# HGRN projections as seven block products for eight over half the rows, and the residual stream kept in DRAM

## The chip, the cores and the metric

One core of one Trainium2 chip runs the whole kernel. The metric is the device time of one execution in microseconds; the kernel before takes 2060.48 us (median of three runs, 2059.94 to 2060.94). TensorE is the matrix engine, VectorE (DVE) and ScalarE (ACT) work element by element, GpSimd (POOL) likewise, and SyncE (SP) issues the loads and stores.

## What is computed

Two layers over 512 tokens of width 2048, in float32. Each is `x <- x + mixer(RMSNorm(x) @ w_in) * silu(z) @ w_out`; the first layer's mixer is a sparse attention (NSA), the second's a gated linear recurrence (HGRN2). A final RMSNorm follows. Only the second layer's projections are changed:

```python
hn = rmsnorm(x, norm_w[layer])
proj = hn @ w_in                     # q, f, i, z: 16 heads x 128 columns each
k = (1.0 - lb) * sigmoid(-f); q = silu(q)
o = recurrence(q, k, i, decay(f)); o = o * rsqrt(mean(o * o)) * gnorm_w
x = x + (o * silu(z)) @ w_out
```

## The kernel before

The weights and activations are float32 and are split into two parts that TensorE takes (`hi` is a rounded copy, `lo` the rest), by `split`: ScalarE casts (L77), VectorE or GpSimd subtracts (L79). Every product of matrices is three: hi by hi, hi by lo, lo by hi. The normalized activations lie transposed as `hhi` and `hlo`, 16 k-tiles of 128 rows by 512 tokens. A *unit* is 128 columns of a projection: f, q or z of one head, or i.

`proj` (L102) makes one unit: for each k-tile three matmuls with 128x128 weights held and all 512 tokens moving (L110 to L112), 48 in all. `proj_pair` (L117) makes f and q of head 0 with 256 tokens at a time (L129 to L131), so that it can start on the first half of the tokens before the second is normalized. `proj_rows` (L134) makes i of two heads, with activations held and 256 weight columns moving (L156 to L158). Weights come by 512 KB loads from SyncE's queue into three `raw` buffers (L83) and are split into rings of four `whi` and four `wlo` buffers of 128x512, each of four k-tiles.

The second layer, `hgrn` (L788), goes over the heads in twos: for each head f and q (`hgrn_levels`, L826, with the decay levels of a head on VectorE, ScalarE and small matmuls `lv`), for each two heads i (`hgrn_inputs`), then the attention and the state (`hgrn_inner`, L960), then z and the gate (`hgrn_gate`, L991). After every four heads `out_proj` (L161) takes their rows of `w_out`: 16 tiles of 128 tokens by 512 columns, 12 matmuls each (L176 to L178), whose sum VectorE adds to x in SBUF (L180). Heads 14 and 15 go side by side at the end.

The turn between the layers: `out_proj_half` (L182 to L200) ends the first layer, first for tiles 0 and 1 of the tokens, then for tiles 2 and 3; after each half `norm` (L352) normalizes these tiles: sums of squares (L341), the reciprocal root (L347 to L349), `xn` (L369 on VectorE, L371 on ScalarE), four transposes by TensorE (L373), `y` (L376) and its split into `hhi` and `hlo`. The tiles `xn` are in the attention's memory.

The order of each engine's instructions isn't written by hand: a scheduler sets it when the kernel is built, from the dependences and the buffers (each `tile_pool`), and each engine then goes through its list in order.

## Time and profile before

| | |
|---|---|
| median of the runs | 2060.48 us |
| span of the profiled execution | 2057.3 us |
| TensorE busy | 2027.9 us, 99 % |
| VectorE busy | 1244.3 us, 60 % |
| ScalarE busy | 862.7 us, 42 % |
| GpSimd busy | 78.9 us, 4 % |
| moved by DMA | 179.83 MB, mean 87 GB/s |

The span is that of one execution under the profiler; the runs are timed without it. The profile gives each engine's instructions with start and length, and, from the semaphores, what each waited for. Matmuls are pipelined: the length of a row overlaps the next row, and the step between two starts is what one costs in a run.

### The profile page before, as it was taken

Reading aid. Unit: us, or ns where it says so; the run is one execution under the profiler, and the core shown is the slowest. Engines: PE = TensorE matmul, PEld = TensorE weight load, DVE = VectorE, ACT = ScalarE, POOL = GpSimd, SP = SyncE. Lnnn points to the kernel's source line nnn. Section 1 sums busy time; section 2 is a strip of 40 time slices with the busy share of each in tenths; the row PEclk is TensorE's granted clock in tenths of the full one; section 3 lists DMA queues with packets and bytes.
Section 4 is the critical chain, followed back from the end, with each engine's and each line's share of the span. In section 5 each row is a group of like instructions: output and inputs, shape, how many; then the busy total and the mean of one; then the engine's idle time right before and its main releaser. Section 6 shows DMA issues by size and latency. Waiting matters only on the chain.

```text
span 2057.3 us, 30342 instructions
## 1 busy us (share of the span) xinstructions
PE 2027.9 (99%) x11666; PEld 1759.2 (86%) x11666; DVE 1244.3 (60%) x2928; ACT 862.7 (42%) x1852; POOL 78.9 (4%) x63
## 2 busy tenths in 40 slices
PE   7999999999999999999999999999999999999997
PEld 7789889888988888889998989889898898988885
DVE  7634676565756575756875656456564565645655
ACT  5223554444535363446733343333432334333344
POOL 5000000000000000001300000000000000000004
PEclk9999999999999999999999999999999999999999
DMA  5353222323232322232423222332322322223233
GB/s 169 82 140 104 72 72 63 92 72 86 60 99 66 92 67 88 62 87 88 155 62 92 73 83 73 92 93 72 93 72 82 97 78 83 73 82 102 77 92 109
DMA packets 272674, 179.83 MB, mean 87 GB/s; under 512 B 8192, under 2 KB 254320, under 8 KB 272528
## 3 DMA queue, kind: packets, MB, share of 16 engines
q1 hardware_dynamic: 272528, 177.88, 29.7%
q8 instruction: 92, 1.51, 0.3%
q14 instruction: 54, 0.44, 0.1%
HBM read 173.66 MB, written 4.19 MB: 86 GB/s over the span
## 4 chain that ended last, share of the span: by engine, by line
PE 95%; DVE 3%; ACT 1%; issue 1%; DMA 0%; SPq 0%; DVEq 0%
PE acc L111 17%; PE acc L110 16%; PE acc L112 16%; PE acc L177 5%; PE acc L176 5%; PE acc L178 4%; PE acc L156 4%; PE acc L157 4%; PE acc L158 4%; PE pt L665 2%; PE lv L951 1%; PE lv L936 1%; PE sc L693 1%; PE sc L691 1%; PE ov L673 1%; PE ov L672 1%
## 5 line engine op out<-in xcount | busy, mean ns | idle before, releaser
L77 ACT CAST whi<-raw 128x512 fp32r<-128x512 f32 x612 | 375.3, 618 | 682.0 <-PE acc L111 455.4
L79 DVE TENSOR_TENSOR wlo<-raw,whi 128x512 fp32r<-128x512 f32 x592 | 409.2, 698 | 392.3 <-ACT whi L77 390.9
L110 PE MATMUL acc<-hhi,whi 128*128 128x512 f32 x1472 | 580.3, 394 | 0.0
L111 PE MATMUL acc<-hlo,whi 128*128 128x512 f32 x1472 | 580.3, 394 | 0.0
L112 PE MATMUL acc<-hhi,wlo 128*128 128x512 f32 x1472 | 579.9, 394 | 0.0
L112 PEld LDWEIGHTS acc<-hhi,wlo 128*128 128x128 f32 x1472 | 276.7, 188 | 58.3
L111 PEld LDWEIGHTS acc<-hlo,whi 128*128 128x128 f32 x1472 | 276.7, 188 | 57.0
L110 PEld LDWEIGHTS acc<-hhi,whi 128*128 128x128 f32 x1472 | 276.8, 188 | 56.2
L156 PE MATMUL acc<-whi,hhi 128*128 128x256 f32 x768 | 217.4, 283 | 0.0
L157 PE MATMUL acc<-wlo,hhi 128*128 128x256 f32 x768 | 216.8, 282 | 0.0
L158 PE MATMUL acc<-whi,hlo 128*128 128x256 f32 x768 | 216.1, 281 | 0.0
L176 PE MATMUL acc<-whi,ohi 128*128 128x512 f32 x416 | 161.7, 397 | 4.2 <-DVE x_all L180 4.1
L177 PE MATMUL acc<-wlo,ohi 128*128 128x512 f32 x416 | 164.2, 395 | 0.0
L178 PE MATMUL acc<-whi,olo 128*128 128x512 f32 x416 | 163.5, 393 | 0.0
L157 PEld LDWEIGHTS acc<-wlo,hhi 128*128 128x128 f32 x768 | 144.8, 189 | 1.1
L156 PEld LDWEIGHTS acc<-whi,hhi 128*128 128x128 f32 x768 | 144.6, 188 | 1.1
L158 PEld LDWEIGHTS acc<-whi,hlo 128*128 128x128 f32 x768 | 144.7, 188 | 0.6
L180 DVE TENSOR_TENSOR x_all<-acc,x_all 128x512 f32<-128x512 f32 x112 | 77.1, 688 | 84.2 <-PE acc L178 83.8
L176 PEld LDWEIGHTS acc<-whi,ohi 128*128 128x128 f32 x416 | 78.4, 189 | 21.2 <-DVE x_all L180 5.3
L714 ACT ACTIVATE p<-p,nm 128x512 f32<-128x512 f32 (+3 forms) x128 | 71.3, 558 | 55.9 <-DVE nm L711 55.3
L177 PEld LDWEIGHTS acc<-wlo,ohi 128*128 128x128 f32 x416 | 78.6, 189 | 17.4 <-DVE wlo L79 2.7
L178 PEld LDWEIGHTS acc<-whi,olo 128*128 128x128 f32 x416 | 78.4, 189 | 16.0
(269 smaller groups left out, 2838.9 us busy)
## 6 DMA issues: line engine op xcount, KB each, us to landing
raw<-in_hgrn_w_in_dram SPq DMA_DIRECT2D x128, 512.0 KB, 4.0
raw<-in_nsa_w_in_dram SPq DMA_DIRECT2D x96, 512.0 KB, 3.7
raw<-in_nsa_w_out_dram SPq DMA_DIRECT2D x40, 512.0 KB, 3.8
raw<-in_hgrn_w_out_dram SPq DMA_DIRECT2D x32, 512.0 KB, 3.8
raw<-in_nsa_w_in_dram SPq DMA_DIRECT2D x32, 256.0 KB, 3.3
out_dram<-x_all SPq DMA_DIRECT2D x16, 256.0 KB, 2.9
x_all<-in_x_dram SPq DMA_DIRECT2D x6, 512.0 KB, 8.2
raw<-in_nsa_ck_w_dram SPq DMA_DIRECT2D x4, 512.0 KB, 4.2
```

The source lines that it names most:

```text
L77: self.nc.scalar.copy(hi, x)
L79: eng.tensor_tensor(out=lo, in0=x, in1=hi.bitcast(F32), op=ALU.subtract)
L110: self.nc.tensor.matmul(acc, hi, self.hhi[:, kt, :], start=first, stop=False)
L111: self.nc.tensor.matmul(acc, hi, self.hlo[:, kt, :], start=False, stop=False)
L112: self.nc.tensor.matmul(acc, lo, self.hhi[:, kt, :], start=False, stop=last)
L156: self.nc.tensor.matmul(acc[:, t, :], self.hhi[:, kt, ts], hi, start=first and t == 0, stop=False)
L157: self.nc.tensor.matmul(acc[:, t, :], self.hhi[:, kt, ts], lo, start=False, stop=False)
L158: self.nc.tensor.matmul(acc[:, t, :], self.hlo[:, kt, ts], hi, start=False, stop=last and t == 1)
L176: nc.tensor.matmul(acc, ohi, hi, start=k == n - 1, stop=False)
L177: nc.tensor.matmul(acc, ohi, lo, start=False, stop=False)
L178: nc.tensor.matmul(acc, olo, hi, start=False, stop=k == 0)
L180: nc.vector.tensor_tensor(out=xs, in0=acc, in1=xs, op=ALU.add)
```

## The change

**Products.** All units of f, q and z but f and q of head 0 are made in pairs by a new `proj_product`: f with q of one head, z with z of the next. Over k-tiles 0 to 7 the work of two units is eight blocks (two halves of the tokens, two halves of the k-tiles, two units); seven products of sums and differences of blocks replace the eight. Each is 12 matmuls of 256 columns. K-tiles 8 to 15 are done as before, in halves of 256 tokens (`rest`). The sums of activations (`forms`) are made once and kept as `fm`; the sums of weights are made for each pair.

```diff
+KP, GAP = 4, 48
+    def forms(self):
+        fm = self.right("forms").tile([128, 4, 2, KP, 256], F32R, name="fm")
...
+        tt(f5, a22[0], a21[0], sub)
+        tt(f5, f5, a22[1], add)
+        tt(f5, f5, a21[1], sub)
...
+        self.fm = {1: raw(0, 0), 2: raw(0, 1), 4: raw(1, 1), 5: made(0), 6: made(1), 3: made(2), 7: made(3)}
+
+    def proj_product(self, w, ca, cb):
...
+        def product(dst, form, wts, start=False, stop=False):
+            (hi, lo), (fhi, flo) = wts, self.fm[form]
+            for k in range(KP):
+                nc.tensor.matmul(dst, hi[:, k], fhi[:, k], start=start and k == 0, stop=False)
+                nc.tensor.matmul(dst, hi[:, k], flo[:, k], start=False, stop=False)
+                nc.tensor.matmul(dst, lo[:, k], fhi[:, k], start=False, stop=stop and k == KP - 1)
...
+        w2, w1 = parts(b21), parts(b11)
+        product(a[:, one], 2, w2, start=True)
+        product(d[:, two], 1, w1, start=True, stop=True)
+        nc.scalar.copy(sa[:, one], d[:, two])
+        t1, t3 = b11, b12
+        add(t1, b11, b12)
+        add(t3, b12, b22)
+        w7 = parts(t3)
+        product(d[:, one], 7, w7, start=True, stop=True)
+        w3 = parts(b22)
+        product(b[:, one], 3, w3, start=True)
+        t2, t4 = b22, b21
+        add(t2, t1, b22)
+        add(t4, t2, b21)
+        w4 = parts(t4)
+        product(a[:, two], 4, w4)
+        w6 = parts(t2)
+        product(d[:, two], 6, w6, start=True, stop=True)
+        add(s2, d[:, two], sa[:, one])
+        add(sa[:, two], d[:, one], s2)
+        rest(a, ca)
+        add(sa, a, sa)
+        w5 = parts(t1)
+        product(d[:, two], 5, w5, start=True, stop=True)
+        add(sb[:, one], d[:, two], s2)
+        add(sb[:, two], d[:, one], sb[:, one])
+        rest(b, cb)
+        nc.vector.tensor_tensor(out=sb, in0=b, in1=sb, op=ALU.subtract)
+        return sa, sb
...
-        acc, accq = self.proj_pair(w_in, cf, cq) if h == 0 else (self.proj(w_in, cf), None)
+        acc, accq = (self.proj_pair if h == 0 else self.proj_product)(w_in, cf, cq)
```

**x in DRAM.** To make room for `fm`, x leaves SBUF when the second layer begins: four stores of 1 MB, issued by GpSimd. For heads 0 to 11 the output projection's tiles are copied by ScalarE and added to x in DRAM by DMA. After the last pair (z of heads 14 and 15, now ahead of their `hgrn_inner`) x is loaded again, 16 pieces of 256 KB.

```diff
             for tiles in ((0, 1), (2, 3)):
                 self.out_proj_half(w_out, 12, last, tiles, self.square_sum)
                 for t in tiles:
+                    nc.gpsimd.dma_start(self.spill[t * 128:(t + 1) * 128, :], self.x_sb[t])
                     self.norm(1, t, pool=self.att)
...
-                xs = self.x_sb[t][:, es]
-                nc.vector.tensor_tensor(out=xs, in0=acc, in1=xs, op=ALU.add)
+                if self.spilled:
+                    y = self.work.tile([128, S], F32, name="yo", tag="tmp", bufs=3)
+                    nc.scalar.copy(y, acc)
+                    nc.gpsimd.dma_start(self.spill[ts, es], y, accum_op=ALU.add)
+                else:
+                    xs = self.x_sb[t][:, es]
+                    nc.vector.tensor_tensor(out=xs, in0=acc, in1=xs, op=ALU.add)
...
+            self.z_pair(w_in, last[0])
+            self.spilled = False
+            self.open_x("xagain")
+            for t in range(NT):
+                for c in range(4):
+                    cs = slice(c * 512, (c + 1) * 512)
+                    nc.gpsimd.dma_start(self.x_sb[t][:, cs], self.spill[t * 128:(t + 1) * 128, cs])
```

**Memory.** The second layer has pools of its own for weights, in memory that the first layer gives back: five `raw` buffers in place of three, `whi` and `wlo` with four as before. In PSUM one bank `pd` for the products takes the place of the second transpose buffer.

**The order at the turn.** The change also moves instructions that it doesn't name. TensorE from the end of the first layer, before (L196 to L198 the last output projection, L129 to L131 the pair of head 0, L373 the second half's transposes; rows left out are of the pair):

```order
L198 MATMUL acc<-whi,olo 128x256
L129 MATMUL acc<-hhi,whi 128x256
L130 MATMUL acc<-hlo,whi 128x256
L131 MATMUL acc<-hhi,wlo 128x256
...
L373 MATMUL pt<-ident,xn 128x128 x8
L131 MATMUL acc<-hhi,olo 128x256
...
L373 MATMUL pt<-ident,xn 128x128 x4
L130 MATMUL acc<-hlo,ohi 128x256
```

and now:

```order
L307 MATMUL acc<-whi,olo 128x256
L495 MATMUL pt<-ident,xn 128x128 x32
L130 MATMUL acc<-hhi,whi 128x256
L131 MATMUL acc<-hlo,whi 128x256
L132 MATMUL acc<-hhi,wlo 128x256
```

Before, 98 matmuls of the pair stand ahead of the last of the 32 transposes; now none does. SyncE's loads of the pair's weights, with what they wait for, before and then now (the loads are the same four):

```order
L83 DMA raw<-in_hgrn_w_in_dram 128x8x128 [waits DMAHW1_49,DVE_49,Pool_49]
L83 DMA raw<-in_hgrn_w_in_dram 128x8x128 [waits DMAHW2_49,DVE_49,Pool_49]
L83 DMA raw<-in_hgrn_w_in_dram 128x8x128 [waits DMAHW3_49,DVE_49,Pool_49]
L83 DMA raw<-in_hgrn_w_in_dram 128x8x128 [waits DMAHW4_49,DVE_49]
```

```order
L84 DMA raw<-in_hgrn_w_in_dram 128x8x128 [waits PE_49,Activation_49]
L84 DMA raw<-in_hgrn_w_in_dram 128x8x128 [waits DVE_49,PE_49]
L84 DMA raw<-in_hgrn_w_in_dram 128x8x128 x2
```

Before, they wait for the splits of earlier weights in the same buffers. Now the PE wait of the first is for the seventh group of transposes of the second half's norm, that of the second for the eighth: the new buffers lie where `xn` was. On VectorE, the subtractions for the pair's weights (`wlo`, `olo`), before, ahead of the second half's norm:

```order
L200 TENSOR_TENSOR x_all<-acc,x_all 128x2x256
L79 TENSOR_TENSOR wlo<-raw,whi 128x512
L79 TENSOR_TENSOR olo<-raw,ohi 128x512 x2
L79 TENSOR_TENSOR wlo<-raw,whi 128x512
L347 TENSOR_REDUCE rs<-ss 128x1 x2
L79 TENSOR_TENSOR olo<-raw,ohi 128x512 x2
L349 RECIPROCAL rs<-rs 128x1 x2
L369 TENSOR_SCALAR xn<-x_all,rs 128x512 x2
```

and now, behind it:

```order
L498 TENSOR_TENSOR y<-pt,nw 128x512
L891 MEMSET ones 128x128
...
L80 TENSOR_TENSOR hlo<-y,hhi 128x4x128
L896 CAST pick_10185<-ones 128x128
L143 TENSOR_TENSOR raw<-hhi 128x1024
...
L80 TENSOR_TENSOR hlo<-y,hhi 128x4x128
...
L80 TENSOR_TENSOR wlo<-raw,whi 128x512
L143 TENSOR_TENSOR raw<-raw,hlo 128x1024
```

Of the pair's eight subtractions (two of its `wlo` stand in the row above the fence's first) all stood ahead of the second half's `xn`; now all come behind its last `hlo`, with operations of the masks (L891 and on) and of `forms` (L143) between them.

## Rows read from the trace of the kernel before

**Rows 1.** The page, parts 1 and 4: busy time of each engine, the chain's shares.

```profile
PE 2027.9 (99%) x11666; PEld 1759.2 (86%) x11666; DVE 1244.3 (60%) x2928; ACT 862.7 (42%) x1852; POOL 78.9 (4%) x63
...
PE 95%; DVE 3%; ACT 1%; issue 1%; DMA 0%; SPq 0%; DVEq 0%
```

**Rows 2.** Stretches: start:end, length, each engine's busy us, PEclk, DMA share, GB/s.

```profile
1140.00:1960.00 820.00, 819.67 (x4735) 706.07 (x4734) 473.57 (x1031) 295.86 (x599) 0.00 (x0) 1.00 0.29 83
...
2005.00:2010.00 5.00, 3.94 (x20) 3.07 (x19) 4.41 (x10) 1.05 (x1) 1.44 (x1) 1.00 0.59 203
2010.00:2015.00 5.00, 2.52 (x12) 1.75 (x10) 3.72 (x4) 2.84 (x5) 3.34 (x2) 1.00 0.30 105
2015.00:2020.00 5.00, 4.49 (x14) 3.64 (x15) 2.38 (x5) 0.81 (x1) 2.41 (x1) 0.66 0.00 0
```

**Rows 3.** TensorE in order of time, a 512-column run: start, length, instruction [idle before].

```profile
1106.83 0.39 PE L112 MATMUL acc<-hhi,wlo 128*128 128x512 f32 x1
...
1114.84 0.39 PE L111 MATMUL acc<-hlo,whi 128*128 128x512 f32 x1
```

**Rows 4.** TensorE in order of time, the unit pair of head 0.

```profile
1035.16 0.28 PE L131 MATMUL acc<-hhi,wlo 128*128 128x256 f32 x1
...
1046.00 0.28 PE L131 MATMUL acc<-hhi,olo 128*128 128x256 f32 x1
```

**Rows 5.** TensorE in order of time: last output projection of layer one, row projection.

```profile
1014.99 0.28 PE L198 MATMUL acc<-whi,olo 128*128 128x256 f32 x1
...
1017.49 0.28 PE L198 MATMUL acc<-whi,olo 128*128 128x256 f32 x1
...
1048.91 0.28 PE L156 MATMUL acc<-whi,hhi 128*128 128x256 f32 x1
...
1051.97 0.28 PE L156 MATMUL acc<-whi,hhi 128*128 128x256 f32 x1
```

**Rows 6.** Groups by line, the page's, then 1040 to 1960; waits, 1040 to 1960 and later.

```profile
L79 DVE TENSOR_TENSOR wlo<-raw,whi 128x512 fp32r<-128x512 f32 x592 | 409.2, 698 | 392.3 <-ACT whi L77 390.9
...
L888 DVE TENSOR_TENSOR K<-K,tot 128x256 f32<-128x256 f32 x91 | 38.1, 419 | 0.1
...
ACT whi L77 <- PE acc L111: 257.2, 136, 3.4
...
PE acc L176 <- DVE x_all L180: 4.1, 2, 3.0
```

**Rows 7.** TensorE in order of time, the turn between the layers.

```profile
1017.61 0.28 PE L129 MATMUL acc<-hhi,whi 128*128 128x256 f32 x1
...
1025.98 1.03 PE L373 MATMUL pt<-ident,xn 128*128 128x128 f32 x8
...
1034.34 0.66 PE L373 MATMUL pt<-ident,xn 128*128 128x128 f32 x4 [0.64 <-DVE y L376]
```

**Rows 8.** VectorE in order of time, the same turn.

```profile
1018.13 0.68 DVE L200 TENSOR_TENSOR x_all<-acc,x_all 128x512 f32<-128x512 f32 x1
...
1024.19 0.88 DVE L369 TENSOR_SCALAR xn<-x_all,rs 128x512 f32<-128x512 f32 x2
1026.62 1.29 DVE L376 TENSOR_TENSOR y<-pt,nw 128x512 f32<-128x512 f32 x2 [1.54 <-PE pt L373]
...
1037.02 1.28 DVE L79 TENSOR_TENSOR hlo<-y,hhi 128x512 fp32r<-128x512 f32 x2
```

**Rows 9.** SyncE's DMA queue in order of time; the page, part 6, KB and us.

```profile
1006.91 11.70 SPq L83 DMA_DIRECT2D raw<-in_hgrn_w_in_dram  x4
...
raw<-in_hgrn_w_in_dram SPq DMA_DIRECT2D x128, 512.0 KB, 4.0
```

**Rows 10.** The page, part 6: other DMA issues, KB each, us to landing.

```profile
out_dram<-x_all SPq DMA_DIRECT2D x16, 256.0 KB, 2.9
x_all<-in_x_dram SPq DMA_DIRECT2D x6, 512.0 KB, 8.2
```

**Rows 11.** Stretches at the start of the kernel, columns as in rows 2.

```profile
4.00:8.00 4.00, 0.28 (x1) 0.18 (x1) 1.78 (x7) 1.68 (x5) 0.99 (x2) 1.00 0.93 255
...
12.00:16.00 4.00, 2.46 (x18) 2.03 (x17) 3.96 (x8) 3.82 (x11) 3.69 (x4) 1.00 1.03 379
```

More of the change, by code (lines that the diff above doesn't have):

```diff
@@ L132, in proj_pair @@
         return units[0][0], units[1][0]
+    def forms(self):
+        nc = self.nc
+        fm = self.right("forms").tile([128, 4, 2, KP, 256], F32R, name="fm")
+        blk = lambda part, t, k: part[:, k * KP:(k + 1) * KP, t * 256:(t + 1) * 256].bitcast(F32)
+        a11, a12, a21, a22 = ([blk(p, t, k) for p in (self.hhi, self.hlo)] for t in range(2) for k in range(2))
+        f5, f6, f3, f7 = (self.rawpool.tile([128, KP, 256], F32, name="raw", tag="raw") for i in range(4))
+        tt = lambda o, a, b, op: nc.vector.tensor_tensor(out=o, in0=a, in1=b, op=op)
+        add, sub = ALU.add, ALU.subtract
+        split = lambda i: self.split((f5, f6, f3, f7)[i], fm[:, i, 0], fm[:, i, 1])
+        tt(f5, a22[0], a21[0], sub)
+        tt(f5, f5, a22[1], add)
+        tt(f5, f5, a21[1], sub)
+        nc.vector.scalar_tensor_tensor(f6, f5, -1.0, a11[0], op0=ALU.mult, op1=sub)
+        tt(f6, f6, a11[1], sub)
+        split(0)
+        tt(f3, f6, a12[0], add)
+        tt(f3, f3, a12[1], add)
+        split(1)
+        split(2)
+        tt(f7, a11[0], a21[0], sub)
+        tt(f7, f7, a11[1], add)
+        tt(f7, f7, a21[1], sub)
+        split(3)
+        raw = lambda t, k: [p[:, k * KP:(k + 1) * KP, t * 256:(t + 1) * 256] for p in (self.hhi, self.hlo)]
+        made = lambda i: [fm[:, i, 0], fm[:, i, 1]]
+        self.fm = {1: raw(0, 0), 2: raw(0, 1), 4: raw(1, 1), 5: made(0), 6: made(1), 3: made(2), 7: made(3)}
@@ new lines, in proj_product, with parts, rest @@
+    def proj_product(self, w, ca, cb):
+        nc = self.nc
+        add = lambda o, a, b: nc.vector.tensor_tensor(out=o, in0=a, in1=b, op=ALU.add)
+        raws = []
+        for c0 in (ca, cb):
+            raw = self.rawpool.tile([128, 2 * KP, 128], F32, name="raw", tag="raw")
+            nc.sync.dma_start(raw, w[:2 * KP * 128, c0:c0 + 128].rearrange("(k p) n -> p k n", p=128))
+            raws.append((raw[:, :KP], raw[:, KP:]))
+        (b11, b21), (b12, b22) = raws
+        def parts(src):
+            hi, lo = (self.wpool.tile([128, KP, 128], F32R, name=t, tag=t, bufs=4) for t in ("whi", "wlo"))
+            self.split(src, hi, lo)
+            return hi, lo
+        def product(dst, form, wts, start=False, stop=False):
[4 more added lines that the diff above has]
+                nc.tensor.matmul(dst, lo[:, k], fhi[:, k], start=False, stop=stop and k == KP - 1)
+        def rest(acc, c0):
+            src = w[2 * KP * 128:, c0:c0 + 128].rearrange("(k p) n -> p k n", p=128)
+            for k, (hi, lo) in enumerate(self.load_split(src, [128, KT - 2 * KP, 128])):
+                kt = 2 * KP + k
+                for ts in (one, two):
+                    stop = kt == KT - 1 and ts is two
+                    nc.tensor.matmul(acc[:, ts], hi, self.hhi[:, kt, ts], start=False, stop=False)
+                    nc.tensor.matmul(acc[:, ts], hi, self.hlo[:, kt, ts], start=False, stop=False)
+                    nc.tensor.matmul(acc[:, ts], lo, self.hhi[:, kt, ts], start=False, stop=stop)
+        one, two = slice(0, 256), slice(256, 512)
+        a = self.pproj.tile([128, S], F32, name="acc", tag="acc")
+        b = self.pproj.tile([128, S], F32, name="acc", tag="acc")
+        d = self.pd.tile([128, S], F32, name="d", tag="d")
+        sa, sb = (self.hp.tile([128, S], F32, name=n, tag=n, bufs=1) for n in ("sa", "sb"))
+        s2 = self.hp.tile([128, 256], F32, name="s2", tag="s2", bufs=1)
+        w2, w1 = parts(b21), parts(b11)
[27 more added lines that the diff above has]
+        return sa, sb
@@ L221, in flip_rows, with right, open_x @@
         self.nc.vector.tensor_copy(dst, p[:, 0, :n])
+    def right(self, name):
+        if self.atright:
+            self.atright.close()
+        self.atright = ExitStack()
+        return self.atright.enter_context(self.tc.tile_pool(name=name, bufs=1, side="right", reuse_waits="tile"))
+    def open_x(self, name="xpool"):
+        if not self.atright:
+            pool = self.tc.tile_pool(name="edge", bufs=1, side="right")
+            self.ctx.enter_context(pool).tile([128, 24], F32, name="edge")
+        self.x_all = self.right(name).tile([128, NT, D], F32, name="x_all")
+        self.x_sb = [self.x_all[:, t, :] for t in range(NT)]
     def setup(self, ncon):
@@ L231, in _setup @@
         nc, consts = self.nc, self.consts
-        self.x_all = consts.tile([128, NT, D], F32, name="x_all")
-        self.x_sb = [self.x_all[:, t, :] for t in range(NT)]
+        self.open_x()
         rows = tmp.tile([2 * KT, 128], F32, name="nwrows")
@@ L435, in rope @@
         nc.scalar.copy(q, acc)
-        sw = self.work.tile([64, S], F32, name="sw", tag="sw", bufs=1)
+        sw = self.ncon.tile([64, S], F32, name="sw", tag="sw", bufs=1)
         nc.vector.stream_shuffle(sw[32:], q[:32], [(i + 16) % 32 for i in range(32)])
```

62 lines of the change are left out of this document (40 added, 22 removed).

## Prediction

> **What bounds the kernel now.** I read the page first, for the busy shares and the chain that ended last; then the stretches, to see whether every stage of the second layer has the same limit; then TensorE in order of time, for the price of one matmul; then the engines beside it and the waits; last the turn from the first layer to the second, and the loads. TensorE is busy 2027.9 us and carries 95 % of the chain [rows 1]. From 1140 to 1960 us, where most of the changed work lies, it idles 0.33 us of 820, with VectorE at 473.57 (58 %) and ScalarE at 295.86 (36 %) [rows 2]. A matmul left out there is time gained, if the extra work fits into VectorE's free 42 %. The profiled execution spans 2057.3 us; the median of the runs is 2060.48, so 3.2 us lie around the span. The sum moves the span; I add it to the median.
>
> **The products.** Two units are 96 matmuls of 512 columns now. A row's own length overlaps the next, so I take starts: 35 unbroken steps from 1106.83 to 1114.84 us, 0.2289 each [rows 3]; 96 x 0.2289 = 21.97 us. After the change they are 7 x 12 = 84 product matmuls and 96 for the other eight k-tiles, 180 of 256 columns. The nearest row for these is the unit pair, which also has weights stationary and 256 tokens moving: 92 steps from 1035.16 to 1046.00, 0.1178 each [rows 4]. 180 x 0.1178 = 21.20 us, 0.77 less. With 23 pairs (f and q of heads 1 to 15, z of eight head pairs): **-17.8 us**. A sixteenth of the columns is gone, which would be 1.37 us a pair, but a half-width matmul costs 0.515 of a full one, and that eats nearly half. Other rows of 256 columns bound it: 21 steps of 0.119 in the last output projection and 27 steps of 0.1133 in the row projection [rows 5] give 0.55 and 1.58 us a pair, 12.6 to 36 us. I take the pair's pace since its operands are the same.
>
> The Trainium skill ("TensorE: Matmul & The Clock Gate", Back-to-back issue gap) gives streams with weight loads 131 ns at 512 columns and 81 ns at 128; on a straight line between them a 256-column matmul would take 98 ns (an estimate), and each pair would be 5 us slower instead of faster. The 228.9 and 117.8 ns steps speak against it, and I give it no chance of its own.
>
> **VectorE beside the products.** A pair now costs it eight splits of 128x512. Afterwards it has eleven splits, four additions of weights and one subtraction and one addition of 512, and four of 256. A 512 split takes 698 ns, one of 256 columns about 420 [rows 6], but two in a row take 1.28 [rows 8], so one more costs 0.60; I put 256 at 0.34 with the same overlap. That is 4.8 us before and 17 x 0.60 + 4 x 0.34 = 11.6 after: 6.8 x 23 = 156 us more, less 48 additions to x that go (29 us). VectorE in this layer rises from 58 to some 72 %: no bound as a mean. By segments of the built order at these prices the fullest, between the ends of two pairs where a head's levels stand beside a pair, holds 21.5 us against TensorE's 23.0. ScalarE gains three casts and a copy a pair and loses nothing; it stays under 50 %.
>
> What is thin is the lead. ScalarE's casts of weights wait for TensorE to free one of four buffers (257.2 us in 136 waits) [rows 6], so they run ahead by the ring alone. One buffer lasts 12 matmuls: 2.75 us before, 1.41 in a product. Three buffers in hand thus cover 4.2 us instead of 8.2, for a cast of 0.62, a split of 0.7 and whatever stands ahead of it on VectorE, whose operations for a head's levels themselves wait for TensorE. Nothing here shows such a wait: below, 0; above, one split's wait (0.7 + 0.62) in most pairs, some 25 us. Nearest is the present kernel, without any: I take +4.
>
> **The turn between the layers.** This is the dearest item. Now the first pair's matmuls start at 1017.61, and 98 of them stand between the last projection and the norm's last transposes, at 1034.34; the pair's last row is at 1046.00 [rows 4, 7]. So the second half's norm is nearly free. In the changed order all 32 transposes stand first. Worse, the four loads of the pair's weights, issued from 1006.91 on now [rows 9], go into memory of the norm's xn tiles: the first waits for the seventh transpose group. From the last addition to x, 1018.13 + 0.68 [rows 8], squares, sum, root and reciprocal take about 2.5 us without the weight casts between them, to 1021.3. VectorE then has four xn (0.40), eight y and eight hlo (0.60 each, from [rows 8]), one 1024-wide form (two steps of 512, 1.2) and short operations for the masks (some 1.3, an estimate), 13.7 us and 1.5 more for the first transposes: the last hlo ends near 1037 and the first wlo near 1038. The weights' loads start near 1029.5, take 4.0 [rows 9] and a cast, so they are no later. The pair's 192 matmuls at 0.1178 are 22.6, and the form between the next wlo may hold them a little: they end near 1061 instead of 1046.1. **+15 us**, 10 if TensorE's first matmuls and the splits overlap better, 20 with the clock: the one drop of the granted clock here, to 0.66 in 2015 to 2020 (1.0 is the 2.4 GHz level), came behind 5 us with TensorE busy for 2.52 [rows 2], and cost up to 1.7 us.
>
> The rest of the forms (1024-wide operations and four splits) then lies before the levels of head 0, while TensorE has the row projection's 192 matmuls: **+2 us**, 0 to 5.
>
> **x through DRAM.** Four stores of 1 MB by GpSimd's queue stand ahead of four to eight of its splits and of two mask operations; the stores' issue alone holds them: 0 to 2, taken 0. Each of 48 tiles of the output projection is copied by ScalarE and added by DMA. Three buffers for tiles of 12 x 0.2289 = 2.75 us give each DMA 8.2 us. No row shows an accumulating DMA, or one issued by GpSimd; a 256 KB store lands in 2.9, and 512 KB loads in the burst at the start in 8.2 [rows 10]. The store is the nearest row, thus 0; a duration of 12 would cost (12 - 8.2) / 3 x 48 = 61 us. The additions that go hid under TensorE but for 4.1 us of waits near the tail [rows 6].
>
> The reload, 4 MB in 16 DMAs, starts when the last product has read the forms. At 379 GB/s, the rate of the start [rows 11], it is 11 us, at 255 16 us. TensorE has 48 x 0.1178 = 5.7 of the rest, two heads' inner work and the first output tiles of 1.37 each, while the tail of now stalls by about 4 us itself (busy 3.94 and 2.52 in two stretches of 5) [rows 2]. Net **0**, -4 to +8.
>
> **Sum:** -17.8 + 4 + 15 + 2 + 0 = +3.2 us, **2063.5 us**. 0.2 %, about what a measurement of this kernel can tell from no change, is 4.1 us, so the forecast itself is "no change", its own range 2053 to 2074.
>
> **The rivals.** *The products run at the row projection's pace* (0.115 on average): 1.27 us a pair, -29 us, and with half the stalls 2050. For it: forms and weights are read in the same 256-column pieces; against: the pair does so too, and is slower. *The weights come late in every pair*: the head's levels on VectorE queue ahead of the wlo, and four buffers of 1.41 us don't cover; at 1 us a pair in place of 0.2 it is +18 more, 2082. It decides from a wait of about 4.2 us in VectorE's queue; for it: 21.5 of 23.0 us in the fullest segment; against: there is none now, and segments of 39 to 41 us of 55. *The accumulating DMA holds the output buffers*: from 8.2 us a DMA on, 12 gives 2125. Against it: loads of twice the size land in 4.0 [rows 9]. The Trainium skill ("SBUF — State Buffer", the trap that DVE blocks DMA) says GpSimd's descriptors wait while VectorE runs an operation of a two-port mode; no row here shows a DMA of GpSimd's. *The change doesn't do what it says* can't be: the built order has the 84 + 96 matmuls in each of 23 pairs. *The turn is cheap* (4 us in place of 15, if the pair starts at 1027): 2052.
>
> **How the numbers follow.** Forecast 0.42, products at the faster pace 0.15, cheap turn 0.10, late weights 0.22, slow DMA 0.08, the rest 0.03 slower. The forecast's range lies about 0.1 faster, 0.2 same and 0.12 slower; of the two fast rivals 0.02 and of the late weights 0.02 end within it. Faster 0.33, same 0.24, slower 0.43. The range takes in the fast rivals' and the late weights' times with their bounds, 2043 to 2088, and leaves out the slow DMA and the far ends.
>
> **What would show it.** The products' rows 0.1178 apart and 21.2 us of matmuls a pair; a gap on TensorE between 1018 and 1038, with transposes alone in it, and the pair's end near 1061; VectorE near 72 % between there and 1960; waits of TensorE for wlo of a few us in all. The forecast is wrong if TensorE's steps are under 0.116, if waits for wlo pass 10 us, if TensorE waits for a copy of an output tile, or if the pair starts before 1030.

## The result and the profile after

The changed kernel takes **2074.86 us** (median of four runs, 2072.67 to 2077.30) against 2060.40 (2059.94 to 2060.94) for the kernel before on the same chip: a ratio of 1.0071, 95% interval 1.0057 to 1.0085, so slower by 14.5 us. The profiled execution spans 2070.9 us, 13.6 more than before. The forecast was 2063.5, the range 2043 to 2088.

First the busy times [rows 1]: TensorE's sum fell by 16 us and its share of the span too, and the time rose. Whatever was lost, was lost in idle time.

```profile
PE 2012.1 (97%) x13598; PEld 1834.8 (89%) x13598; DVE 1375.6 (66%) x3193; ACT 937.4 (45%) x1994; POOL 130.0 (6%) x131
```

Then the same stretches as in [rows 2], with the same columns: start:end, length, busy us of PE, PEld, DVE, ACT and POOL, PEclk, DMA share, GB/s. The long stretch had 0.33 us without TensorE and has 13.2 now. In the tail there are five microseconds in which TensorE does nothing, at a DMA share of 0.88 and half the clock.

```profile
1140.00:1960.00 820.00, 806.82 (x6404) 769.46 (x6403) 573.67 (x1257) 364.08 (x730) 41.51 (x48) 1.00 0.40 100
2005.00:2010.00 5.00, 0.00 (x0) 0.00 (x0) 2.84 (x1) 4.41 (x13) 4.52 (x4) 0.51 0.88 333
2010.00:2015.00 5.00, 2.69 (x9) 2.44 (x10) 4.96 (x10) 0.56 (x2) 1.23 (x1) 0.50 0.36 116
2015.00:2020.00 5.00, 5.00 (x32) 4.39 (x31) 3.59 (x7) 2.95 (x7) 2.39 (x1) 0.97 0.14 47
```

TensorE in order of time shows three of the places (start, length, instruction, idle before it and its releaser). At the turn the first layer's last matmul is at 1020.27; then come transposes in pieces, and the first pair's matmuls only from 1036.09 to 1061.84, where [rows 4, 7] have 1017.61 to 1046.00. The run from 1120.04 to 1142.03 is 193 unbroken steps of 256 columns, products and `rest`: 0.1139 us each. At 2002.50 the tail stops.

```profile
1020.27 0.28 PE L307 MATMUL acc<-whi,olo 128*128 128x256 f32 x1
1023.90 1.09 PE L495 MATMUL pt<-ident,xn 128*128 128x128 f32 x8 [3.35 <-ACT xn L493]
...
1036.09 0.58 PE L130 MATMUL acc<-hhi,whi 128*128 128x256 f32 x1 [3.91 <-ACT whi L78]
...
1038.36 0.58 PE L132 MATMUL acc<-hhi,wlo 128*128 128x256 f32 x1 [1.48 <-DVE wlo L80]
...
1061.84 0.28 PE L132 MATMUL acc<-hhi,olo 128*128 128x256 f32 x1
...
1120.04 0.39 PE L188 MATMUL d<-fm,whi 128*128 128x256 f32 x1
...
1142.03 0.28 PE L199 MATMUL acc<-hlo,whi 128*128 128x256 f32 x1
...
2002.50 0.39 PE L282 MATMUL acc<-whi,olo 128*128 128x512 f32 x1
2012.31 1.65 PE L1109 MATMUL sp<-I,KT 128*128 128x128 f32 x6 [9.42 <-DVE KT L74]
```

The waits of TensorE (us in all, times, longest), from 1140 to 1960, and last the longest of the tail, from 1971 to 2040. `sa` is the copy of a product by ScalarE, `KT` the transposed K that the state's matmuls `sp` take:

```profile
PE lv L1090 <- DVE K L1027: 5.1, 6, 0.9
PE acc L188 <- ACT whi L78: 4.5, 6, 1.3
PE lv L1090 <- ACT attT L1092: 2.1, 6, 0.3
PE d L188 <- ACT sa L211: 1.4, 6, 0.2
...
PE sp L1109 <- DVE KT L74: 9.4, 1, 9.4
```

What stands behind the 9.4 us is read from the other engines in order of time. GpSimd issues the 16 loads that bring x back from 1992.72 on. SyncE issues w_out's weights at 1995.51, and ScalarE's cast of them waits 9.01 us for the landing, 10 us behind the issue; the median of the 32 loads of w_out is 4.0 (last row, from the page). VectorE's split behind it takes 4.63 us instead of 0.70 [rows 6] while GpSimd's two splits run beside it; then comes the copy of KT, for which TensorE waits.

```profile
1992.72 5.44 POOL L947 DMA_DIRECT2D x_all<-xd  x10 [120.06 <-PE d L190]
...
1995.51 16.67 SPq L517 DMA_DIRECT2D raw<-in_hgrn_w_out_dram  x2
...
2005.56 1.04 ACT L78 CAST hhi<-raw 128x1024 fp32r<-128x1024 f32 x1 [9.01 <-DMA raw<-in_hgrn_w_out_dram]
...
2006.58 4.65 POOL L80 TENSOR_TENSOR hlo<-raw,hhi 128x1024 fp32r<-128x1024 f32 x2
...
2007.16 4.63 DVE L80 TENSOR_TENSOR wlo<-raw,whi 128x512 fp32r<-128x512 f32 x1 [7.74 <-ACT whi L78]
2011.71 0.54 DVE L74 COPY KT<-pt 128x384 f32<-128x384 f32 x1
...
raw<-in_hgrn_w_out_dram SPq DMA_DIRECT2D x32, 512.0 KB, 4.0
```

The rest of this trace bears the split out: of VectorE's 128x512 splits, 682 had no GpSimd operation beside them and took at most 1.10 us; 24 beside one of GpSimd's splits took up to 1.78, and this one, beside two in a row, 4.63.

The Trainium skill ("GPSIMD Engine Reference", Key points) says that GpSimd shares its SBUF interfaces with VectorE and contends with its instructions of two SBUF inputs; this split has two, and the two rows of 4.6 us agree.

Four points of time, taken from TensorE's rows, put the 14 us in place:

| us | before | after | difference of the stage |
|---|---|---|---|
| last matmul of the first layer | 1017.49 | 1020.27 | +2.8 |
| first matmul behind the first rows | 1072.26 | 1087.63 | +12.6 |
| last matmul of the last rows | 1965.86 | 1971.43 | -9.8 (the heads) |
| first matmul of the last projection | 2025.20 | 2038.90 | +8.1 (the tail) |

The heads gave back 9.8 us. The first layer's end, the turn and the tail took 23.5.

### The profile page after: what moved, and what is told of

Read it like the earlier page. It is cut to its first block, busy times and chain, and to the rows that moved or that the text cites. A ratio compares the mean times of both kernels' runs of the same rounds, so it can differ in the third digit from the quotient of the medians.

```text
span 2070.9 us, 34906 instructions
## 1 busy us (share of the span) xinstructions
PE 2012.1 (97%) x13598; PEld 1834.8 (89%) x13598; DVE 1375.6 (66%) x3193; ACT 937.4 (45%) x1994; POOL 130.0 (6%) x131
## 4 chain that ended last, share of the span: by engine, by line
PE 67%; issue 25%; DVE 4%; POOL 2%; ACT 1%; DMA 1%; SPq 0%; DVEq 0%; POOLq 0%; ACTq 0%
PE acc L113 8%; PE acc L112 8%; PE acc L111 8%; PE acc L261 3%; PE acc L262 3%; PE acc L260 3%; PE acc L280 3%; PE acc L281 3%; PE acc L282 3%; PE acc L199 2%; PE acc L198 2%; PE acc L200 2%; PE pt L788 2%; POOL xd L286 2%; DVE hlo L80 1%
## 5 line engine op out<-in xcount | busy, mean ns | idle before, releaser
L80 DVE TENSOR_TENSOR wlo<-raw,whi 128x512 fp32r<-128x512 f32 x661 | 455.4, 701 | 347.8 <-ACT whi L78 343.2
L78 ACT CAST whi<-raw 128x512 fp32r<-128x512 f32 x681 | 411.3, 618 | 581.3 <-PE acc L112 187.5
L113 PE MATMUL acc<-hhi,wlo 128*128 128x512 f32 x736 | 288.7, 392 | 0.0
L112 PE MATMUL acc<-hlo,whi 128*128 128x512 f32 x736 | 288.3, 392 | 0.0
L111 PE MATMUL acc<-hhi,whi 128*128 128x512 f32 x736 | 288.1, 391 | 0.0
L199 PE MATMUL acc<-hlo,whi 128*128 128x256 f32 x736 | 205.7, 279 | 0.0
L200 PE MATMUL acc<-hhi,wlo 128*128 128x256 f32 x736 | 205.3, 279 | 0.0
L198 PE MATMUL acc<-hhi,whi 128*128 128x256 f32 x736 | 205.2, 279 | 0.0
L111 PEld LDWEIGHTS acc<-hhi,whi 128*128 128x128 f32 x736 | 138.3, 188 | 27.2
```

What stands on the lines that cost most here:

```text
L78: self.nc.scalar.copy(hi, x)
L80: eng.tensor_tensor(out=lo, in0=x, in1=hi.bitcast(F32), op=ALU.subtract)
L111: self.nc.tensor.matmul(acc, hi, self.hhi[:, kt, :], start=first, stop=False)
L112: self.nc.tensor.matmul(acc, hi, self.hlo[:, kt, :], start=False, stop=False)
L113: self.nc.tensor.matmul(acc, lo, self.hhi[:, kt, :], start=False, stop=last)
L198: nc.tensor.matmul(acc[:, ts], hi, self.hhi[:, kt, ts], start=False, stop=False)
```

## The experiments

Twelve runs, each beside the kernel before (2059.1 to 2060.5). Four asked where each stage's time went, eight whether it can be had back.

**1. Are the loads late at the turn?** The two heads' tiles are split into two pools, so that the buffers of the first pair's weights no longer lie on the norm's tiles.

```diff
-            self.hp = hp = es.enter_context(tc.tile_pool(name="hg", reuse_waits="tile", bufs=2))
+            near = es.enter_context(tc.tile_pool(name="hga", reuse_waits="tile", bufs=2))
             self.rawpool = es.enter_context(tc.tile_pool(name="raw5", reuse_waits="tile", bufs=5))
+            self.hp = hp = Pools(near, es.enter_context(tc.tile_pool(name="hg", reuse_waits="tile", bufs=2)))
```

> Only the place of the second layer's buffers is changed: the first pair's weight loads no longer lie on the norm's xn tiles, and each engine's order stays. Theory (the order costs the turn, since all eight wlo and olo stand behind the last hlo on VectorE, 1037.6 us): the pair still ends within 2 us of 1062, the time within 3 us of the changed kernel's 2074.9. Rival (the late loads cost it): the pair ends at 1055 or before, the time falls by 5 us or more, below 2070.

Measured: 2076.08 us, 1.0078 [1.0063, 1.0093]. The loads were issued 24 us sooner, at 1007.26 instead of 1031.12, and the pair still ended at 1062.95. They are not the cause.

```profile
1007.26 4.94 SPq L92 DMA_DIRECT2D raw<-in_hgrn_w_in_dram  x4
...
1062.95 0.28 PE L140 MATMUL acc<-hhi,olo 128*128 128x256 f32 x1
```

**2. Is it the order?** The weights' and three raw buffers are laid out ahead of both layers; the scheduler then puts the pair behind the first layer's last matmul, as before the change.

```diff
+        t.wpool = ctx.enter_context(tc.tile_pool(name="weights", bufs=4))
+        t.rawpool = Raws(ctx.enter_context(tc.tile_pool(name="raw3", bufs=3)))
...
-            self.wpool = es.enter_context(tc.tile_pool(name="weights2", reuse_waits="tile", bufs=4))
-            self.rawpool = es.enter_context(tc.tile_pool(name="raw5", reuse_waits="tile", bufs=5))
+            self.rawpool.more(es.enter_context(tc.tile_pool(name="raw2", reuse_waits="tile", bufs=2)))
```

> The weight buffers of the first layer are kept for the second (three raw buffers, two more behind the turn), so that the scheduler puts 98 matmuls of the first pair ahead of the last transposes again, as in the kernel before. Theory (the order at the turn costs 15 us): the pair ends near 1048 instead of 1062, the granted clock stays at 1.00 there, the time falls by 12 to 15 us to about 2061. Rival (the forms' 1024-wide operations are the cost and only come later): the first product starts as late as now, near 1087, and the time falls by 5 us or less.

Measured: 2091.29 us, 1.0153 [1.0138, 1.0168]. In order of time on TensorE, the pair's last row, the rows' first and the first product's:

```profile
1049.50 0.28 PE L145 MATMUL acc<-hhi,olo 128*128 128x256 f32 x1
...
1055.42 0.79 PE L273 MATMUL acc<-whi,hhi 128*128 128x256 f32 x2 [5.64 <-ACT whi L91]
...
1087.01 0.28 PE L201 MATMUL acc<-hhi,whi 128*128 128x256 f32 x1
```

The pair moved as the theory said, and the gain was gone at the first product: the rows' loads were issued only at 1049.59, since the forms held the raw buffers. And something new: the heads took 19 us longer with the same work and nearly the same waits. The matmuls themselves were slower, a step of 0.1197 us on average in the products and `rest` against 0.1151.

**3. The reload in steps.** Four steps of 1 MB, each held by a tiny copy until the one before has landed.

```diff
-            for t in range(NT):
-                for c in range(4):
+            for c in range(4):
+                if c:
+                    nc.gpsimd.tensor_copy(self.x_all[:, :, c * 512:c * 512 + 1],
+                                          self.x_all[:, :, c * 512 - 512:c * 512 - 511])
+                for t in range(NT):
```

> x is loaded again in four steps of 1 MB, a column block each, and each step waits until the one before has landed. Theory (the reload of 4 MB in one burst starves the load of the last rows of w_out, 10 us instead of 4, and ScalarE's queue waits on it): ScalarE's wait of 9.0 us and TensorE's of 9.4 us near 2005 go, the time falls by 8 to 11 us to about 2065. Rival (x itself comes too late whatever its order): TensorE then waits for additions to x by as much, and the time is within 3 us of 2074.9.

Measured: 2071.16 us, 1.0055 [1.0040, 1.0070], 3.7 us below the changed kernel. The wait for KT fell from 9.4 to 4.8 us, and w_out's load landed 5.2 us behind its issue instead of 10:

```profile
2001.80 9.60 SPq L517 DMA_DIRECT2D raw<-in_hgrn_w_out_dram  x3
...
2006.99 1.04 ACT L78 CAST hhi<-raw 128x1024 fp32r<-128x1024 f32 x1 [6.57 <-DMA raw<-in_hgrn_w_out_dram]
```

The reload in one burst delays w_out's load; about half the wait has that cause alone. The edit touches nothing before the reload, and yet the heads took 887.9 us in this trace, 885.3 in run 1's and 883.8 in the changed kernel's: a stage of one trace can differ by some 4 us without a cause in the edit (the last section has more).

**4. Eight products for eight.** 192 half-width matmuls a pair, no forms, no sums of weights; all else as changed.

```diff
-        product(a[:, one], 2, w2, start=True)
...
+                for k, (hi, lo) in enumerate(self.proj_weights(w, c0, c)):
+                    for ts in (slice(0, 256), slice(256, 512)):
+                        self.nc.tensor.matmul(acc[:, ts], hi, self.hlo[:, kt, ts], start=False, stop=False)
```

> The pairs and x in DRAM stay, but each pair is computed with all 192 matmuls of 256 columns, without forms and without sums of weights. Theory (the twelve matmuls a pair are worth 12 x 0.1155 = 1.39 us, and the 13 us of waits in the heads come from VectorE's extra work): TensorE's busy time from 1140 to 1960 is without waits, the stretch of the heads is longer by 32 - 13 = 19 us, the end without the reload's wait shorter by 9: about 2085. Rival (the waits come from the smaller lead of 256-column work, whatever VectorE does): they stay above 8 us, and the time is above 2092.

Measured: 2097.58 us, 1.0183 [1.0166, 1.0200]. The pair ended at 1061.30 and the first projection behind the rows began at 1087.74, within 0.6 us of the changed kernel: in this order the forms cost nothing at the turn. The heads took 916.3 us against 883.8. Of these 32.5 us the 22 pairs' own matmuls are 25.8, waits left out: that is what seven products for eight are worth here, 1.17 a pair. Most of the rest is `out_proj`, 5.2, and the row projections, 2.3. The long stretch has this:

```profile
1140.00:1960.00 820.00, 808.98 (x6403) 772.41 (x6402) 432.01 (x954) 312.62 (x625) 51.24 (x64) 1.00 0.41 102
```

VectorE has 142 us less to do there. The 7.2 us of the levels' waits are gone, and 11 us of other waits stand in their place, for weights (7.7) and for a copy of an output tile (2.9). So the run doesn't tell whether the levels waited for VectorE's load as such. The reload, which no forms hold back here, was issued between 1846.6 and 1909.3, long before w_out's last loads: the tail is 59.9 us (67.5 in the changed kernel), without a wait for KT.

**5. Does the place of the weights set the step?** One number, by which the second layer's weights start 64 bytes lower.

```diff
-KP, GAP = 4, 48
+KP, GAP = 4, 32
```

> The changed kernel with one number changed: the unused tile ahead of the second layer's weights is 128 bytes a partition instead of 192, so that the weights (and what lies behind them) start 64 bytes lower, at an even multiple of 64 bytes as in the run with the old turn; order and instructions stay. Theory (where the weights lie sets the step of the matmuls, which was 0.1198 us on average in that run against 0.1152 in the changed kernel): the step of the 256-column matmuls between 1040 and 2010 us becomes 0.119 to 0.120, the heads take some 19 us longer, 2094 us in all. Rival (the slow step came with the other order, not with the place): 0.115 to 0.116, and 2073 to 2078 us.

Measured: 2097.16 us, 1.0181 [1.0165, 1.0196]; 22.3 us for 64 bytes. The same run of 193 steps as at 1120.04 above:

```profile
1123.31 0.39 PE L188 MATMUL d<-fm,whi 128*128 128x256 f32 x1
...
1146.57 0.28 PE L199 MATMUL acc<-hlo,whi 128*128 128x256 f32 x1
```

23.26 / 193 = 0.1205 us against 0.1139. The theory held. (The buffers behind the weights moved too; in runs 2, 6 and 9 these lie otherwise, and the step goes with the weights.) From 1140 to 1960 the waits (12.7 us) and the granted clock (1.00) are those of the changed kernel.

**6 and 7. The turn mended**, without and with the stepped reload. To run 2 come 64 bytes of padding ahead of the weights, and the forms move behind the rows.

```diff
+        ctx.enter_context(tc.tile_pool(name="pad", bufs=1)).tile([128, 16], F32, name="pad")
         t.wpool = ctx.enter_context(tc.tile_pool(name="weights", bufs=4))
...
-                    if i == 0:
-                        self.forms()
                     if i == h:
                         inputs = self.hgrn_inputs(w_in, h)
+                    if i == 0:
+                        self.forms()
```

> The run with the old turn (second layer's weights and three raw buffers laid out ahead of both layers, so the scheduler puts the pair behind the last projection of the first layer again) with two things added: 64 bytes of padding ahead of the weights, and the forms called after the rows of the first two heads, so that the rows' loads no longer wait for raw buffers that the forms hold. Theory (the turn's 15 us are the order's and not the forms'; the slow step was the place's): pair ends near 1047, rows start at once, first product near 1073 (1087.6 in the changed kernel), heads as in the changed kernel (884 us), so 15 us less: 2060 us. Rival 1 (the forms, some 25 us of VectorE, come last whatever the order): first product 1080 to 1087, 2068 to 2075 us. Rival 2 (the place is not what made the step slow): first product as in the theory, but heads of 900 us: 2076 us or more.

> The same with the stepped reload of x added (four steps of 1 MB). The two gains lie in different stages, so they should add: 3.7 us below the run before it, 2056 us if the theory there holds, and then below the kernel before the change (2060.4). Rival (with the turn mended the end of the heads runs into the reload in another way): no gain over it.

Measured: 2076.69 us, 1.0082 [1.0067, 1.0097], and 2075.98 us, 1.0079 [1.0062, 1.0096]. Both misses, and for a reason in neither expectation: the first layer ended at 1030.21, 10 us late. The pad moved its weights too, and there the projections' matmuls of 512 columns took 0.2333 us a step, against 0.2278, over some 2070. From that end to the first product it was 52.1 us instead of 67.4, so the turn gained its 15; 8 of them went again before the next rows, where VectorE, full of forms, held the levels and TensorE ran at a granted clock of 0.66 for 10 us:

```profile
1087.00:1097.00 10.00, 9.60 (x48) 8.93 (x49) 7.44 (x18) 4.13 (x8) 0.00 (x0) 0.66 0.01 2
```

The stepped reload gained nothing certain here: a wait for `o` of 4.5 us stood beside the one for KT of 4.2.

**8. Two operations off VectorE.** The scalings of f and K at the head of each head's levels go to ScalarE.

```diff
-        nc.vector.tensor_scalar(f, f, oml, lb, op0=ALU.mult, op1=ALU.add)
-        nc.vector.tensor_scalar(K, K, oml, None, op0=ALU.mult)
+        nc.scalar.activation(f, f, AF.Identity, scale=oml, bias=lb)
+        nc.scalar.activation(K, K, AF.Copy, scale=oml)
```

> The changed kernel with the two scalings of f and K at the head of each unit's levels (one VectorE operation of 128x512 each, two a head, 32 in all) done by ScalarE instead. Theory (the 13.2 us of waits between 1140 and 1960 us, 7 of them of the levels' matmuls and of the units' matmuls for VectorE's work, come from the load of VectorE, 70 per cent busy there): waits fall by a third or more, and the time by 4 us or more, to 2071 or less. Rival (they come from the order in which the queues were written, as the run with eight products suggested, where 11 us were left with VectorE at 53 per cent): the waits change place, not sum, 2073 to 2079 us.

Measured: 2067.20 us, 1.0039 [1.0024, 1.0054], 7.7 us below the changed kernel. The long stretch, and all that is left of its waits:

```profile
1140.00:1960.00 820.00, 813.26 (x6440) 776.52 (x6439) 565.61 (x1232) 382.73 (x759) 41.52 (x48) 1.00 0.40 101
```

```profile
PE acc L188 <- ACT whi L78: 5.2, 6, 1.8
PE acc L188 <- ACT ohi L78: 0.9, 6, 0.2
```

The levels' waits (5.1 + 2.1) are gone, those for weights stayed. VectorE is busy 69 % here against 70, so its sum of work hardly changed; what changed is a head's chain on VectorE, two operations shorter now. That the length of this chain, and not the load, is what TensorE waited for fits both this run and run 4, where the chain is shorter too, but no run has the one without the other. In the tail nothing was gained for sure (66.0 us against 67.5): w_out's load is as late, 9.6 us from issue to landing, and TensorE waits 9.0 us for additions to x instead.

**9 and 10. All that held, together**, with the stepped reload, and with another: the loads of x for each 512 columns issued by SyncE behind w_out's. whi and wlo become slices of one tile of both layers, 64 bytes higher in the second.

```diff
+    def weight(self, shape, tag):
...
+        a = 2048 * i + 512 * n + 16 * self.spilled_once
+        return self.wbig[:, a:a + 512].rearrange("p (k n) -> p k n", n=shape[1])[:, :shape[0]]
```

> All parts that held, together: the old order at the turn, forms after the rows, the scalings on ScalarE, the stepped reload; and whi and wlo now lie in one tile that both layers share, at an even multiple of 64 bytes in the first layer and 64 bytes higher, at an odd one, in the second. In the run with the mended turn the pad had moved them in both layers: the end of the first layer came 10 us later there (1030.2 against 1020.3), where the mean step of the 512-column matmuls was 0.2342 us against 0.2290 over 2240 of them. Theory (whether whi and wlo lie at an even or an odd multiple of 64 bytes sets the step, and the better side differs between 512-column and 256-column steps): the first layer ends near 1020.5 with steps of 0.229, products' steps stay at 0.115; time 2076.7 less 10 less 7.7 less 1 to 4 = 2055 to 2058 us, below the kernel before the change (2059 to 2060). Rival 1 (the first layer was late from the other things that the pad moved): it ends near 1030, 2065 to 2068 us. Rival 2 (parts overlap: the scalings' gain was in the waits of the turn and at the end, which the other order has mended already): 2060 to 2064 us.

> The same with another reload of x instead of the stepped one: the four loads of each 512-column block are issued by SyncE behind the loads of w_out of the same block in the last out_proj, so they come after these in the queue and not before them. Theory (the reload costs the tail because 4 MB come ahead of w_out's first load): the wait of the last heads' chain for w_out goes, the tail (last rows to last projection) falls from some 67 us to 60, and the time is 3 to 6 us below the stepped reload's. Rival (the additions of the last projections now wait for x, which comes later): the wait moves to the additions on VectorE and to PE for a PSUM buffer, no gain or some us slower.

Measured: **2054.84 us, 0.9974 [0.9963, 0.9984]**, and 2054.86 us, 0.9973 [0.9963, 0.9984]: both faster than the kernel before, by 5.3 us, and than the changed one by 20. Of run 9 the long stretch and the tail's:

```profile
1140.00:1960.00 820.00, 813.60 (x6462) 774.67 (x6460) 563.67 (x1238) 370.94 (x749) 41.75 (x48) 1.00 0.41 101
2000.00:2020.00 20.00, 19.54 (x94) 15.97 (x93) 14.25 (x25) 5.71 (x16) 6.31 (x9) 1.00 0.33 107
```

The tail (last row of the rows to the last projection) is 58.7 us, before the change 59.3. Steps alone had left it at 62.4 (run 3), the scalings alone at 66.0 (run 8); together they end it, so they don't add up one by one. Run 10's reload gave 58.8 and nothing more: with the wait for KT gone there was nothing left for it to win.

The number came out at the edge of what was expected (2055 to 2058), and one reason did not: the first layer ended at 1026.30, not 1020.5. And this order has a price of its own: from the first product to the second rows it is 76.1 us, against 70.0 in the changed kernel.

**11 and 12. Where the six microseconds are.** The first layer's projections were back at 0.2279 a step, but its `out_proj` had 0.2333 where the changed kernel has 0.2286. Run 11 moves ohi and olo by 64 bytes; run 12 puts them into the shared tile.

```diff
-        t.wbig = ctx.enter_context(tc.tile_pool(name="wbig", bufs=1)).tile([128, 4112], F32R, name="wbig")
+        t.wbig = ctx.enter_context(tc.tile_pool(name="wbig", bufs=1)).tile([128, 4128], F32R, name="wbig")
```

```diff
-        i = ("whi", "wlo").index(tag)
+        i = ("whi", "wlo", "ohi", "olo").index(tag)
```

> The version that beat both kernels with 64 bytes more in the shared weights' tile, so that ohi and olo, which lay at an odd multiple of 64 bytes there in both layers, lie at an even one. In that version the first layer still ended at 1026.3 us, 6 us later than in the changed kernel, with the 512-column steps whose weights are whi and wlo back at 0.229 but those that stream them past ohi and olo at 0.2345 to 0.2358, against 0.2293 to 0.2304. Theory (the place of the operands again, now of ohi and olo): those steps become 0.230, the first layer ends some 4 to 6 us sooner, near 1021 to 1022, and the time is 2049 to 2051 us, unless the last projections of the second layer, whose step was 0.2300, now lose as much as 2 us. Rival (the six us come from the queues' order or waits in the first layer and not from steps): the end of the first layer stays near 1026, 2054 to 2056 us.

> The version that beat both kernels, with ohi and olo in the shared tile too, so that all four move together: whi and ohi lie 16384 bytes apart in both layers, as in the changed kernel. Up to here the 512-column steps that pair ohi or olo with whi or wlo took 0.229 to 0.231 us wherever the distance was 16384 bytes (the changed kernel; the version that beat both, second layer: 0.2300) and 0.234 to 0.236 where it was 16448 or 16512 (that version's first layer; the last run in both layers, 0.2354 in the second), so evenness was not the rule for these. Theory (the distance between the two operands decides): 0.229 to 0.231 in both layers, the first layer ends between 1020.5 and 1022.5, 2049 to 2051 us. Rival (no such rule; each layout has its own steps): a first layer that ends near 1026 or a second one with steps of 0.235, 2054 to 2060 us.

Run 11: 2060.28 us, 0.9998 [0.9989, 1.0007]; the theory of even multiples fell. The first layer ended at 1027.39, and the second one's `out_proj` slowed as well. Its run of 45 steps from 1319.03 takes 10.50 us, 0.2333 each:

```profile
1319.03 0.39 PE L303 MATMUL acc<-wbig,ohi 128*128 128x512 f32 x1
...
1329.53 0.40 PE L304 MATMUL acc<-wbig,olo 128*128 128x512 f32 x1
```

The same run in the version of run 9 takes 10.23 us, 0.2273 each:

```profile
1317.00 0.39 PE L303 MATMUL acc<-wbig,ohi 128*128 128x512 f32 x1
...
1327.23 0.39 PE L304 MATMUL acc<-wbig,olo 128*128 128x512 f32 x1
```

Steps are not the whole of the six: up to the half projections run 9 is 6.7 us behind the changed kernel, with 4.2 more in `out_proj`'s matmuls, 4.1 more in waits and 1.6 less in the other matmuls.

Run 12 goes round its ring of four for ohi and olo in the order in which the code is written, so some heads' values take the place of ones that the output projection has not used yet. Its first layer ends at 1051.13, with 19 us of waits (5.5 for weights, 3.7 for pcs), and its 2079.67 us, 1.0096 [1.0079, 1.0113], is no time of this kernel. Its steps can be read: 0.2282 and 0.2275 in the two layers. Over the runs, mean steps from start to start; longer ones than 0.25 us at 512 columns and 0.14 at 256, where other work comes between, are left out (the expectations' means, by another count, are up to 0.002 higher). Some 2070, 3900, 510 and 630 of each:

| run | whi from ohi, bytes, layer 1 / 2 | proj 512, layer 1 | products and `rest` 256, layer 2 | out_proj 512, layer 1 / 2 |
|---|---|---|---|---|
| changed kernel | 16384 / 16384 | 0.2278 | 0.1151 | 0.2286 / 0.2277 |
| 5, second layer 64 lower | 16384 / 16384 | 0.2278 | 0.1198 | 0.2286 / 0.2279 |
| 6, first layer 64 higher | 16384 / 16384 | 0.2333 | 0.1151 | 0.2287 / 0.2279 |
| 9 | 16448 / 16384 | 0.2279 | 0.1148 | 0.2333 / 0.2274 |
| 11 | 16512 / 16448 | 0.2279 | 0.1148 | 0.2329 / 0.2333 |
| 12 | 16384 / 16384 | 0.2278 | 0.1150 | 0.2282 / 0.2275 |

The row of run 6 is against its neighbour run 2, which has 0.2278 and 0.1197. For `out_proj` the distance of the two operands fits all six rows; that it, and not a place of its own, decides is shown by no run apart.

## Why the prediction was right or wrong

The range held the result, but the likeliest case did not come: "no change" was forecast, and the kernel is slower by 0.7 %. The terms, in us:

| term | predicted | measured |
|---|---|---|
| products | -17.8 | -21.1, and -1.9 in the heads' other matmuls |
| late weights and levels, 1140 to 1960 | +4 | +13.2 |
| turn | +15 | +12.6, and +2.8 in the first layer's end |
| forms | +2 | 0 |
| x through DRAM and the tail | 0 | +8.1 |
| sum | +3.2 | +13.7 |

That the time stayed within the range is partly luck: the matmuls gave 5 us more than forecast and hid part of what the stalls, the tail and the first layer's end cost more.

**The tail is the step that failed.** "The reload ... Net 0, -4 to +8" set the reload's 11 to 16 us against TensorE's own work and left out who else needs the DMA engines just then: w_out's load, issued 3 us behind it, landed 10 us after its issue instead of the 4.0 of its group, and the chain of casts, split and KT stood behind that. The upper bound was about right. Runs 3, 4, 9 and 10, with the reload in steps, earlier or later, show that it can be had back.

**The stalls were mis-sized.** "Nearest is the present kernel, without any: I take +4." I measured 13.2. Late weights are 4.5 of it, as taken, and the rival "the weights come late in every pair" (1 us a pair) did not come. What the sum lacks are the 7.2 of the levels' matmuls, 5.1 for VectorE's chain and 2.1 for a copy by ScalarE, and 1.4 for ScalarE's copy of a product. A check by sums over a segment (21.5 of 23.0 us) can't see a chain.

**The products gained more than predicted.** Between the two points of the heads, 22 pairs before and now (the 23rd lies in the tail), the pairs' rows on TensorE add up to 492.0 us and 470.9, waits left out: 21.1 less, 0.96 a pair where I had 0.77. Row projections took 2.8 less with the same work, the small matmuls 1.1 more. The unbroken steps average 0.1151, so the rival "at the row projection's pace" (0.115) named the step, and the forecast's own sign of being wrong, steps under 0.116, came. The pair's 0.1178 was taken "since its operands are the same", and it is only one of the values that the same work can have: the pair of head 0 steps at 0.1134 in the changed kernel and at 0.1178 in run 1, with the same instructions and weights in the same place (last section). Where the weights lie matters as well, and the layout was part of the change: in that of run 5 the matmuls step at 0.1198 and the change costs 38 us in all (2097.16 against 2059.10).

**The turn was right, by its own steps.** First wlo near 1038: 1037.62. Loads near 1029.5: 1031.12. Pair's end near 1061: 1061.84. The clock did fall, to 0.86 from 1018 to 1038 and 0.91 from there to 1062: up to 1042.4 the pair's steps are 0.213, 2.3 us more than at 0.1134. That the times agree so well is partly luck, since the forecast had the first layer end at 1017.49 and not 2.8 later; the faster steps and a shorter norm made up for that and the clock. Runs 1, 2, 4 and 6 show that the order costs this, not the loads, and that the forms cost nothing beside it. With the old order and the forms behind the rows (runs 6 and 9) 6 to 8 us go before the second rows; whether to the forms was not tried apart.

**The accumulating DMA** was no bound: 48 of them landed in 5.4 us (median; the longest took 7.1), under the 8.2 that three buffers allow, and TensorE never waited for a copy of an output tile between 1140 and 1960.

```profile
xd<-yo POOLq DMA_DIRECT2D x48, 256.0 KB, 5.4
...
x_all<-xd POOLq DMA_DIRECT2D x16, 256.0 KB, 6.8
```

The first layer's +2.8 was not in the sum at all: about 1.0 of it is there when the half projections begin (957.50 against 956.45), the rest comes within them, beside GpSimd's stores. That these cause it was not tried.

## What to carry to other kernels

A change that saves matmuls is paid at the ends of the stage: look there for what it puts next to whom, above all for a bulk transfer that meets a small load on the path. Where a layout moves, measure the step of the matmuls again before anything else is explained: 64 bytes were worth 22 us here, more than the change itself. Compare a stage between two traces that it should not differ in before a few us are read from it: here that gave up to 4. And a sum of an engine's work over a stretch bounds nothing while another engine waits for a chain on it.

## What the hardware showed unexpectedly

Matmul steps of equal instructions come in several sizes, at full granted clock. At 256 columns there are three: 0.1134, 0.1178 and 0.1200 us. In the heads seven stretches of some 193 steps are unbroken. With the weights where run 5 has them, all seven step at 0.1200, but for the first step of each. Where the changed kernel has them, 64 bytes higher, a stretch keeps to one of the other two, and which one changes from trace to trace without an edit to it: in the changed kernel all seven are at 0.1134, in run 1 and in run 3 two of the seven are at 0.1178, which makes 0.85 us more each. The same stretch in the changed kernel and then in run 1, 192 steps of 0.1134 and of 0.1178:

```profile
1224.04 0.29 PE L189 MATMUL d<-fm,whi 128*128 128x256 f32 x1
...
1245.81 0.28 PE L199 MATMUL acc<-hlo,whi 128*128 128x256 f32 x1
```

```profile
1225.36 0.28 PE L197 MATMUL d<-fm,whi 128*128 128x256 f32 x1
...
1247.97 0.28 PE L207 MATMUL acc<-hlo,whi 128*128 128x256 f32 x1
```

Between the heads of run 3 and of the changed kernel the pairs' matmuls differ by 3.0 of the 4.1 us, the waits by 1.1; what chooses between the two sizes is open. At 512 columns the out_proj runs above have 0.2273 and 0.2333 (45 steps). Moving the operands by 64 bytes switches between fast and slow, and 512 and 256 columns of the same pair of tiles preferred opposite places (run 6 against run 2: 0.2333 and 0.1151 against 0.2278 and 0.1197). Which addresses make which step is open.

VectorE's split of 512 columns took 4.63 us instead of 0.70 beside two of GpSimd's splits, and waited out both. And after the idle 10 us of the tail TensorE was granted 0.50, the lower of its two levels, until about 2015: the first 512-column matmuls there start 0.43 to 0.57 us apart.
